# Half of each projection slot moved between a pair's two V sums, and three more weight units kept in a ring buffer

## The chip, the cores and the metric

The kernel runs on one NeuronCore of a Trainium2 chip. The metric is the device time of one execution in microseconds; the time of a kernel is the median of its runs.

## The reference

A decoder trunk of four layers works on 256 tokens of width 1024, all in float32. Layer by layer the mixer is HGRN2, FoX (softmax attention with a forget gate), Mamba-2 SSD, and HGRN2 again. Behind each mixer stands a PEER feed-forward: for each token, 8 heads pick 16 of 16384 experts by a product of keys, and each expert is one row of a table `u` and one row of a table `v`.

```python
def block(xb):                       # 128 tokens
    q = (xb @ w_q).reshape(M, 8, 2, 128)
    ...                              # top 16 of 128 x 128 sums of key scores, softmax gates
    u = jnp.take(u_tab, idx, axis=0) # (M, 8, 16, 1024)
    v = jnp.take(v_tab, idx, axis=0)
    act = gelu(einsum('md,mhkd->mhk', xb, u)) * gates
    return einsum('mhk,mhkd->md', act, v)
...
h = h + mixer(rmsnorm(h, norm_mix[i]))   # w_in, then a recurrence or attention, then w_out
h = h + peer_ffn(rmsnorm(h, norm_ffn[i]), ...)
```

So 256 tokens x 4 layers x 128 rows of 8 KB (`u` and `v` stand beside each other in memory) are gathered, 1.07 GB, and each mixer and each query projection has its weights besides.

## The kernel before

The work of one layer is split into two halves of the tokens, t=0 and t=1. There are eight stages, s = 0 to 7: stage s does the PEER of layer s//2, half s%2, and beside it, as "side work", the mixer and the queries of the next half (`side(s)` runs `ready(s + 1)`). Stage 2 thus has the FoX mixer for t=1 beside it, stage 3 the SSD mixer for t=0, stage 6 the second HGRN2 mixer for t=1.

**Pairs.** A stage has 64 pairs, 512 in all. A pair i is two gathers, g=0 and g=1. One gather (L1848, issued by POOL) brings 128 rows of 8 KB, 1 MB, into a buffer of the "ring". VectorE multiplies its `u` half with the tokens and sums (`dot`), ScalarE makes the activation and the scaled diagonal matrix (`active`: Gelu, then `dg`), and TensorE adds the `v` half into PSUM: the "V sum" (`spread`, L1919), two matmuls for each of g=0 and g=1. Behind its V sum the buffer is free, and a further gather may be issued into it. The ring holds six buffers of `gb` and, after the opening, a seventh, `GB[6]`; buffers that held kept weights join it when their weights are done.

**Weights.** A weight matrix is cut into units of 1 MB (128 x 2048 float32). `stream` lists them in the order of use, each once for t=0 and once for t=1. A unit loaded into one of NRAW = 2 `raw` buffers is loaded for both halves of the tokens. A unit named in `KEEP` goes into a kept place (`spots`, numbers 0 to 8: eight units of `kept` and the end of `mix`) and stays there for t=1. `look_ahead` and `given_back` take a kept place out of the ring when its unit is near in the stream, and hand it back when the unit has been used for the last time. Kept mixer units are loaded by a DMA that ScalarE issues (`paced`, at most PACE = 4 units ahead of use), all others by one that SyncE issues.

**The side work's slots.** A `Plan` lists for each slot n what TensorE does (`pe`) and what the other engines do behind it (`at`). `halves(ns, gen)` puts two half units of an in-projection (`project`, four matmuls of 128x512 in the order, two to a half) into one slot. `run(most)` cuts a slot in two when more than `most` us of TensorE work (3.0 for HGRN2 and FoX, 99 for SSD) by the kernel's own count have been put into it. In the main loop a pair is written in this order: `dot(i,0)`, `active(i,0)`, `spread(i,0)`, `dot(i,1)`, `active(i,1)`, `spread(i,1)`, steps of the routing, the other engines' part of the last slot (`others`), and then the next slot's TensorE work (`products_`). The next slot is taken while the counted cost is behind the line `SIDE[s] * slot / SPAN`. Engines run their instructions in the order in which they are written.

Of the kernel before, what the change touches and what calls it, by code (L numbers as in the profile page):

```python
# [26 lines left out]
UNIT = 2048  # L27
# [7 lines left out]
MIX = 10304  # L35
STAGES = 2 * DEPTH

def in_order(*units):
    return {i: k for k, i in enumerate(units)}


FIRST = in_order(*range(9))
KEEP = {"hg0": in_order(0, 1, 2, 6, 7, 8, 9, 10, 11), "hg1": {**in_order(*range(7), 8, 9), 18: 3, 19: 4}, "fox": {**in_order(0, *range(2, 10)), 15: 2},
        "ssm": {**in_order(*range(8)), 31: 0}, "wq0": in_order(3, 4, 5, 6, 1, 2, 7), "wq1": {3: 0, 4: 1, 1: 3, 2: 4, 0: 5, 5: 6, 6: 7, 7: 8},
        "wq2": {0: 1, 3: 2, 1: 3, 2: 4, 4: 5, 5: 6, 6: 7}, "wq3": {3: 0, 0: 1, 4: 2, 1: 5, 2: 6, 5: 7, 6: 8, 7: 3}}
PARKED = ({("wq0", 1): 7, ("wq0", 2): 8}, {("fox", 15): 3, ("wq1", 1): 4, ("wq1", 2): 5, ("wq1", 0): 6},
          {("ssm", 31): 0, ("wq2", 0): 1, ("wq2", 1): 3, ("wq2", 2): 4},
# [11 lines left out]
NKEPT = 8  # L59
# [146 lines left out]
def trunk(ctx: ExitStack, tc: tile.TileContext, d: dict, out: bass.AP):  # L206
# [19 lines left out]
    at_, o_ = {}, 0  # L226
# [100 lines left out]
    over = set()  # L327
    order.reverse()

    spots = [at_["kept"][:, k * UNIT:(k + 1) * UNIT] for k in range(NKEPT)] + [mix[:, MIX - UNIT:]]  # L330
    ring = deque(GB[:6])
    vacant, wanted = set(range(NKEPT + 1)), set()

# [193 lines left out]
    class Plan:  # L527
        def __init__(self):
            self.slots = {}
            self.holds = {}  # L530

        def hold(self, n, until):

# [10 lines left out]
        def halves(self, ns, gen):  # L544

            for n in ns:
                for _ in range(2):
                    self.pe(n, lambda: next(gen))

        def run(self, most):  # L550

            for n in range(max(self.slots) + 1):
                ps, fs = self.slots.get(n, ((), ()))
                while n in self.holds and routed[0] < self.holds[n]:
                    yield "wait"
                start = pe[0]
                for i, f in enumerate(ps):
                    if i and pe[0] - start > most:
                        yield
                        flush()  # L560
                        yield
                        start = pe[0]
                    f()
                yield from slot(lambda: deferred.extend(fs))

    def turned(src, use, n=4, twisted=False):

# [82 lines left out]
    def hgrn(l, t, carry):  # L650
# [147 lines left out]

        p = Plan()
        nm = "hg%d" % j  # L800
        p.halves(range(16), project(nm, ub, ["f0", "f1", "q0", "q1", "v0", "v1", "g0", "g1"]))
        if t and l:
            p.at(1, unpark, ("wq3", 0))
        p.at(1, bounds)
# [390 lines left out]
    def fox(l, t, carry):  # L1195
# [78 lines left out]
            later(lambda: nc.scalar.copy(YT[:, j], b[:, 0:P]))  # L1274

        p = Plan()
        p.halves(range(12), project("fox", ub, ["v0", "v1", "q0", "k0", "q1", "k1"]))
        p.pe(0, gate[0])
        for n in range(1, 8):
            p.at(n, lambda: next(gate[1], None))  # L1280
# [22 lines left out]
    def ssd(l, t, carry):  # L1303
# [185 lines left out]
        ins = [n for n in range(11) for _ in range(2)] + [11, 12, 13, 14, 15, 16, 17, 17, 18, 18]  # L1489
        ins += [19, 19, 20, 20, 21, 21, 22, 23, 24, 24, 25, 26, 27, 27, 28, 28]  # L1490
        gen = project("ssm", ub, list(range(8)) + ["z%d" % g for g in range(4)])
        for n in ins:
            p.pe(n, lambda: next(gen))
        p.at(0, setup)
        p.pe(1, gate[0])
        for n in range(2, 9):
# [554 lines left out]
    for s in range(STAGES):  # L2051
# [1 line left out]

            ring.extend(mix[:, (3 + 2 * i) * D:(5 + 2 * i) * D] for i in range(3))
        work = side(s) if s else chain(first, side(0))
        state = {"open": False, "done": False, "pe": 0.0, "dve": 0.0, "cost": 0.0, "slot": 0}

        def products_(force=False):

            state["slot"] += 1  # L2060
            if state["done"] or not (force or state["cost"] < SIDE[s] * state["slot"] / SPAN):
                return
            state["pe"], state["dve"] = pe[0], dve[0]
            r = next(work, work)
            state["done"] = r is work
            state["open"] = r is None
            state["pe"] = pe[0] - state["pe"]
            state["dve"] = dve[0] - state["dve"]

        def others():  # L2070

            if state["open"]:
                d0 = dve[0]
                next(work)
                state["open"] = False
                state["cost"] += max(state["pe"] / 4.6, (state["dve"] + dve[0] - d0) / 2.2, 0.5)

        for i in range(64 * s, 64 * s + 64):
# [9 lines left out]
            elif new:  # L2088

                products_(True)  # L2090
                others()
            spread(i, 0)
            if i:
                dot(i, 1)
            active(i, 1)
# [45 lines left out]
```

## Time and profile before

| | |
|---|---|
| median of 3 runs | 3025.08 us (3023.35 to 3025.86) |
| the profiled execution | 3023.55 us, of which the instructions span 3021.8 us |
| TensorE (PE), VectorE (DVE), ScalarE (ACT), GpSimd (POOL) busy | 82%, 70%, 52%, 40% |
| DMA engines | busy share 9 tenths or more in 37 of 40 slices, mean 417 GB/s |
| moved | 1259.48 MB, of it 1073.81 MB by gathers |
| ACT's table loads | 318, 1283 ns each |

The page's second part shows busy tenths in 40 slices of the span (75.5 us each) and, for the DMA engines, the GB/s that they moved. A row of a view by windows gives busy time and count of each engine, then the granted TensorE clock, the DMA engines' busy share and GB/s. A "dry spell" is here a stretch in which the GB/s fall below the 427 of a stretch with work always waiting.

### The profile page before, as it was taken

To read this page: it belongs to the slowest core of one execution; us is meant where nothing else is said; L and a number is where in the kernel's file an instruction comes from. 1 tells how busy PE (TensorE), PEld (TensorE's weight loads), DVE (VectorE), ACT (ScalarE), POOL (GpSimd) and SP (SyncE) were. 2 spreads that over 40 slices of the span, in tenths; PEclk is the share of its full clock that TensorE was granted. 3 is DMA by queue.
4 is the path that set the end of the run, shared out by engine and by line. 5 is a ranking of instruction groups with operands and counts; after the bars stand their busy time and mean duration, and the time that the engine had idled before them with its cause. 6 is when DMAs were issued, how large, how long until landed. Compare 5 with 4: busy or idle time off the path is not lost.

```text
span 3021.8 us, 35257 instructions
## 1 busy us (share of the span) xinstructions
PE 2491.9 (82%) x10583; PEld 1076.3 (36%) x10584; DVE 2123.0 (70%) x5664; ACT 1564.1 (52%) x4469; POOL 1214.9 (40%) x1040
## 2 busy tenths in 40 slices
PE   9898787887688986988779998878776888887778
PEld 7544342233134451333233443533222333431111
DVE  3877577675856867778487886787657667787755
ACT  3565444463445744577346774456444654453433
POOL 0443343444443433333344333334334443555554
PEclk9999888988799997998979999889888999999999
DMA  8899999999999999999999999999999999999998
GB/s 365 335 426 426 427 426 427 423 411 426 426 425 408 423 426 427 414 416 417 416 425 409 415 426 427 422 422 422 427 426 426 411 418 421 419 426 427 427 427 360
DMA packets 176637, 1259.48 MB, mean 417 GB/s; under 512 B 19777, under 2 KB 20161, under 8 KB 25538
## 3 DMA queue, kind: packets, MB, share of 16 engines
q0 software_dynamic: 147776, 1073.81, 84.9%
q1 hardware_dynamic: 24786, 156.13, 12.4%
q10 hardware_dynamic: 3888, 27.30, 2.2%
q8 instruction: 87, 1.43, 0.2%
q14 instruction: 100, 0.82, 0.1%
HBM read 1256.11 MB, written 1.05 MB: 416 GB/s over the span
## 4 chain that ended last, share of the span: by engine, by line
DMA 53%; PE 22%; DVE 12%; issue 7%; ACT 3%; POOL 2%; POOLq 0%; SPq 0%; DVEq 0%; ACTq 0%
DMA arena<-in_uv,ix 51%; PE pj L289 11%; DVE arena L248 8%; PE acc L1919 7%; PE ps L289 4%; POOL arena L1848 2%; DMA raw<-in_ssm 2%; ACT L261 1%; DVE eq L248 1%; ACT dg L261 1%; DVE af L248 1%; PE ps L293 1%; ACT arena L261 0%; DVE si L248 0%; DVE gs L248 0%
## 5 line engine op out<-in xcount | busy, mean ns | idle before, releaser
L1848 POOL DMA_INDIRECT arena<-in_uv,ix x1028 | 1209.5, 1177 | 1790.6 <-PE acc L1919 862.3
L248 DVE SCALAR_TENSOR_TENSOR arena<-arena 128x1024 f32<-128x1024 f32 (+2 forms) x1088 | 1265.4, 1172 | 729.1 <-DMA arena<-in_uv,ix 718.4
L1919 PE MATMUL acc<-arena,dg 128*64 128x512 f32 x4096 | 1275.3, 681 | 482.0 <-ACT dg L261 479.7
L1919 PEld LDWEIGHTS acc<-arena,dg 128*64 128x64 f32 x4096 | 285.0, 146 | 1266.3 <-ACT dg L261 985.1
L261 ACT ACTIVATE dots<-dots 128x1 f32<-128x1 f32 x896 | 177.6, 198 | 1002.0 <-DVE arena L248 999.6
L289 PE MATMUL pj<-arena 128*128 128x128 f32 (+2 forms) x2160 | 484.6, 388 | 4.7 <-DVE arena L248 4.5
L261 ACT ACT_TABLE_LOAD x318 | 408.0, 1283 | 13.4 <-DVE arena L248 6.4
L261 ACT ACTIVATE dg<-dg,dots 128x64 f32<-128x64 f32 x1024 | 356.2, 348 | 33.3
L289 PEld LDWEIGHTS pj<-arena 128*128 128x128 f32 (+1 forms) x2160 | 286.2, 190 | 201.7 <-issue 186.4
L289 PE MATMUL pj<-raw,arena 128*128 128x512 f32 (+1 forms) x736 | 313.5, 628 | 24.5 <-DMA raw<-in_ssm 20.0
L261 ACT ACTIVATE dg<-m,gs 128x64 f32<-128x64 f32 x1024 | 294.2, 335 | 1.5 <-DVE gs L248 0.8
L289 PE MATMUL ps<-arena 128*128 128x128 f32 (+5 forms) x1632 | 209.7, 282 | 1.1 <-DMA arena<-in_wq 0.7
L289 PEld LDWEIGHTS ps<-arena 128*128 128x128 f32 (+3 forms) x1632 | 170.9, 177 | 97.1 <-issue 42.7
L289 PEld LDWEIGHTS pj<-raw,arena 128*128 128x128 f32 (+1 forms) x736 | 116.0, 185 | 222.4 <-issue 183.3
L289 PE MATMUL ps<-cst,arena 128*64 128x128 f32 (+4 forms) x960 | 133.4, 321 | 5.2 <-DVE arena L248 5.2
L289 PEld LDWEIGHTS ps<-cst,arena 128*64 128x64 f32 (+1 forms) x960 | 105.7, 182 | 51.8 <-issue 32.6
L261 ACT ACTIVATE dots<-dots,rts 128x1 f32<-128x1 f32 x128 | 37.1, 290 | 137.5 <-DVE arena L248 137.4
L248 DVE DVE_READ_ACCUMULATOR arena<-arena 128x1 f32 x1024 | 84.9, 83 | 0.0
L261 ACT ACTIVATE arena<-arena 128x512 f32<-128x512 f32 (+3 forms) x88 | 49.2, 576 | 55.7 <-DVE arena L248 52.2
L261 ACT ACTIVATE arena<-ps 128x256 f32<-128x256 f32 (+3 forms) x168 | 58.5, 389 | 24.9 <-PE ps L289 24.2
L248 DVE FIND_INDEX8 si<-sv,arena 128x8 uint32<-128x128 f32 x254 | 69.3, 285 | 0.0
L293 PE MATMUL ps<-cst,arena 128*128 128x128 f32 x360 | 62.9, 299 | 3.6 <-DVE arena L248 2.4
(173 smaller groups left out, 1456.6 us busy)
## 6 DMA issues: line engine op xcount, KB each, us to landing
raw<-in_ssm SPq DMA_DIRECT2D x44, 1024.0 KB, 9.1
raw<-in_hg SPq DMA_DIRECT2D x24, 1024.0 KB, 8.9
arena<-in_hg SPq DMA_DIRECT2D x22, 1024.0 KB, 17.3
arena<-in_wq SPq DMA_DIRECT2D x20, 1024.0 KB, 9.0
arena<-in_uv,ix POOLq DMA_INDIRECT x1028, 14.5
raw<-in_wq SPq DMA_DIRECT2D x10, 1024.0 KB, 12.3
raw<-in_fox SPq DMA_DIRECT2D x10, 1024.0 KB, 9.4
arena<-in_fox ACTq DMA_DIRECT2D x9, 1024.0 KB, 9.3
```

Of the source, the lines that this page charges most:

```text
L248: return getattr(nc.vector, name)(o, *a, **k)
L261: nc.scalar.activation(o, i, f, **k)
L289: nc.tensor.matmul(o, w, m, start=start, stop=stop)
L293: nc.tensor.transpose(o, i, ident)
L1848: nc.gpsimd.indirect_dma_start(o, None, src, bass.IndirectOffsetOnAxis(ap=ix, axis=0))
L1919: nc.tensor.matmul(accs[s][e][o:o + 64], dg[:, k], v, start=hh == 0 and q == 0, stop=hh == 7 and q == NQ - 1)
```

## The change

It has two parts. First, of the two half units of an in-projection slot, the first (from slot 1 on) is no longer written in the slot, but between `spread(i, 0)` and `dot(i, 1)` of the pair ahead of it; the second stays where it was. In HGRN2 and FoX this leaves less in the slot, so `run(3.0)` cuts fewer slots in two. Second, `GB[6]` becomes place 9 for one kept unit in each of three mixers: unit 10 of FoX, unit 9 of SSD, unit 10 of the second HGRN2. While such a unit is there, the ring has one buffer less.

```diff
-KEEP = {... "hg1": {**in_order(*range(7), 8, 9), 18: 3, 19: 4}, "fox": {**in_order(0, *range(2, 10)), 15: 2},
-        "ssm": {**in_order(*range(8)), 31: 0}, ...
+KEEP = {... "hg1": {**in_order(*range(7), 8, 9), 10: 9, 18: 3, 19: 4}, "fox": {**in_order(0, *range(2, 11)), 15: 2},
+        "ssm": {**in_order(*range(8)), 9: 9, 31: 0}, ...
...
-    spots = [... for k in range(NKEPT)] + [mix[:, MIX - UNIT:]]
+    spots = [... for k in range(NKEPT)] + [mix[:, MIX - UNIT:], GB[6]]
...
+        def project(self, ns, gen):
+            for k, n in enumerate(ns):
+                if n and n not in ns[:k]:
+                    self.ahead[n] = lambda: next(gen)
+                else:
+                    self.pe(n, lambda: next(gen))
...   (Plan.run)
-                yield from slot(lambda: deferred.extend(fs))
+                deferred.extend(fs)
+                if n + 1 in self.ahead:
+                    yield "ahead"
+                    self.ahead[n + 1]()
+                yield
+                flush()
+                yield
...   (HGRN2; FoX and SSD alike)
-        p.halves(range(16), project(nm, ub, [...]))
+        p.project([n for n in range(16) for _ in range(2)], project(nm, ub, [...]))
...   (main loop)
+        def ahead():
+            if state["ahead"]:
+                p0 = pe[0]
+                next(work)
+                state["ahead"] = False
+                state["pe"] += pe[0] - p0
...
             spread(i, 0)
+            ahead()
             if i:
                 dot(i, 1)
```

What this does to the order shows in three places. In the rows, `acc<-arena,dg` is a V sum (x4 is a whole pair, x2 one half of it), `pj<-arena` 128x512 a projection (x2 is one half unit), `ps` all other TensorE work of the side; V sums are L1919 before and L1933 in the change.

TensorE, the beginning of the SSD in-projection for t=0 (stage 3), before:

```order
491 L1919 MATMUL acc<-arena,dg 64x512 x4
492 L289 MATMUL pj<-arena 128x512 x4
493 L1919 MATMUL acc<-arena,dg 64x512 x4
494 L289 MATMUL pj<-arena 128x512 x4
495 L289 MATMUL ps<-par,arena 128x32 x8
496 L1919 MATMUL acc<-arena,dg 64x512 x4
497 L289 MATMUL pj<-arena 128x512 x4
```

and the same place in the change:

```order
544 L1933 MATMUL acc<-arena,dg 64x512 x4
545 L289 MATMUL pj<-arena 128x512 x4
546 L1933 MATMUL acc<-arena,dg 64x512 x2
547 L289 MATMUL pj<-arena 128x512 x2
548 L1933 MATMUL acc<-arena,dg 64x512 x2
549 L289 MATMUL pj<-arena 128x512 x2
550 L289 MATMUL ps<-par,arena 128x32 x8
551 L1933 MATMUL acc<-arena,dg 64x512 x2
552 L289 MATMUL pj<-arena 128x512 x2
```

Two of the four projection matmuls have moved in front of the pair's second V sum.

TensorE, the beginning of the second HGRN2's in-projection for t=1 (stage 6), before:

```order
957 L1919 MATMUL acc<-arena,dg 64x512 x4
958 L289 MATMUL pj<-arena 128x512 x4
959 L1919 MATMUL acc<-arena,dg 64x512 x4
960 L289 MATMUL pj<-arena 128x512 x4
961 L1919 MATMUL acc<-arena,dg 64x512 x4
962 L289 MATMUL ps<-cst,arena 128x128 x8
963 L289 MATMUL pj<-arena 128x512 x4
964 L1919 MATMUL acc<-arena,dg 64x512 x4
965 L289 MATMUL ps<-arena 128x128 x16
966 L1919 MATMUL acc<-arena,dg 64x512 x4
967 L289 MATMUL pj<-arena 128x512 x4
```

and in the change:

```order
1123 L1933 MATMUL acc<-arena,dg 64x512 x4
1124 L289 MATMUL pj<-arena 128x512 x4
1125 L1933 MATMUL acc<-arena,dg 64x512 x2
1126 L289 MATMUL pj<-arena 128x512 x2
1127 L1933 MATMUL acc<-arena,dg 64x512 x2
1128 L289 MATMUL pj<-arena 128x512 x2
1129 L1933 MATMUL acc<-arena,dg 64x512 x2
1130 L289 MATMUL pj<-arena 128x512 x2
1131 L1933 MATMUL acc<-arena,dg 64x512 x2
1132 L289 MATMUL ps<-cst,arena 128x128 x8
1133 L289 MATMUL pj<-arena 128x512 x2
1134 L289 MATMUL ps<-arena 128x128 x16
```

The work of rows 962 to 967 took two slots with a pair between them; rows 1132 to 1134 are one slot. From here to the first 32x32 products of this mixer there are 16 pairs before and 11 in the change.

SyncE, the weight loads around FoX, t=0 and then t=1, as a difference (`raw` is a buffer for one use, `arena` anything else, `in_wq` query weights, `in_keys` the keys):

```order
-L1975 DMA arena<-in_keys 128x1024
-L443 DMA raw<-in_fox 128x2048 x5
+L1989 DMA arena<-in_keys 128x1024
+L443 DMA raw<-in_fox 128x2048 x4
 L441 DMA arena<-in_fox 128x1024 x2
 L441 DMA arena<-in_wq 128x1024 x2
 L443 DMA raw<-in_wq 128x2048 x2
 L443 DMA arena<-in_wq 128x2048 x2
-L1592 DMA arena<-in_keys 128x1024
-L443 DMA raw<-in_fox 128x2048 x2
+L1606 DMA arena<-in_keys 128x1024
+L443 DMA raw<-in_fox 128x2048
```

One load of 1 MB is gone in t=0 (ScalarE issues it now, so its DMAs go from 27 to 30 over the three mixers) and one in t=1 (nobody issues it). In all SyncE's DMAs go from 174 to 168. ScalarE's table loads go from 318 to 335, since other functions stand between its Gelus; the matmuls are the same number.

More of the change, by code (lines that the diff above doesn't have):

```diff
@@ L42 @@
 FIRST = in_order(*range(9))
-KEEP = {"hg0": in_order(0, 1, 2, 6, 7, 8, 9, 10, 11), "hg1": {**in_order(*range(7), 8, 9), 18: 3, 19: 4}, "fox": {**in_order(0, *range(2, 10)), 15: 2},
-        "ssm": {**in_order(*range(8)), 31: 0}, "wq0": in_order(3, 4, 5, 6, 1, 2, 7), "wq1": {3: 0, 4: 1, 1: 3, 2: 4, 0: 5, 5: 6, 6: 7, 7: 8},
+KEEP = {"hg0": in_order(0, 1, 2, 6, 7, 8, 9, 10, 11), "hg1": {**in_order(*range(7), 8, 9), 10: 9, 18: 3, 19: 4}, "fox": {**in_order(0, *range(2, 11)), 15: 2},
+        "ssm": {**in_order(*range(8)), 9: 9, 31: 0}, "wq0": in_order(3, 4, 5, 6, 1, 2, 7), "wq1": {3: 0, 4: 1, 1: 3, 2: 4, 0: 5, 5: 6, 6: 7, 7: 8},
         "wq2": {0: 1, 3: 2, 1: 3, 2: 4, 4: 5, 5: 6, 6: 7}, "wq3": {3: 0, 0: 1, 4: 2, 1: 5, 2: 6, 5: 7, 6: 8, 7: 3}}
@@ L328, in trunk @@
     order.reverse()
-    spots = [at_["kept"][:, k * UNIT:(k + 1) * UNIT] for k in range(NKEPT)] + [mix[:, MIX - UNIT:]]
+    spots = [at_["kept"][:, k * UNIT:(k + 1) * UNIT] for k in range(NKEPT)] + [mix[:, MIX - UNIT:], GB[6]]
     ring = deque(GB[:6])
@@ L530, in __init__ @@
             self.holds = {}
+            self.ahead = {}
         def hold(self, n, until):
@@ L800, in hgrn @@
         nm = "hg%d" % j
-        p.halves(range(16), project(nm, ub, ["f0", "f1", "q0", "q1", "v0", "v1", "g0", "g1"]))
+        p.project([n for n in range(16) for _ in range(2)], project(nm, ub, ["f0", "f1", "q0", "q1", "v0", "v1", "g0", "g1"]))
         if t and l:
@@ L1276, in fox @@
         p = Plan()
-        p.halves(range(12), project("fox", ub, ["v0", "v1", "q0", "k0", "q1", "k1"]))
+        p.project([n for n in range(12) for _ in range(2)], project("fox", ub, ["v0", "v1", "q0", "k0", "q1", "k1"]))
         p.pe(0, gate[0])
@@ L1491, in ssd @@
         gen = project("ssm", ub, list(range(8)) + ["z%d" % g for g in range(4)])
-        for n in ins:
-            p.pe(n, lambda: next(gen))
+        p.project(ins, gen)
         p.at(0, setup)
@@ L2055, in trunk @@
         work = side(s) if s else chain(first, side(0))
-        state = {"open": False, "done": False, "pe": 0.0, "dve": 0.0, "cost": 0.0, "slot": 0}
+        state = {"open": False, "done": False, "ahead": False, "pe": 0.0, "dve": 0.0, "cost": 0.0, "slot": 0}
         def products_(force=False):
@@ L2065, in products_ @@
             state["done"] = r is work
-            state["open"] = r is None
+            state["ahead"] = r == "ahead"
+            state["open"] = r is None or state["ahead"]
             state["pe"] = pe[0] - state["pe"]
             state["dve"] = dve[0] - state["dve"]
+        def ahead():
[4 more added lines that the diff above has]
+                state["pe"] += pe[0] - p0
         def others():
+            ahead()
             if state["open"]:
@@ L2092, in trunk @@
             spread(i, 0)
+            ahead()
             if i:
```

## The prediction

> **What bounds the kernel now.** I read first the page's slices and queues, then the chain that ended last, then stretches of the span by windows, and at last who waits for whom.
>
> ```profile
> span 3021.8 us, 35257 instructions
> ...
> PE 2491.9 (82%) x10583; PEld 1076.3 (36%) x10584; DVE 2123.0 (70%) x5664; ACT 1564.1 (52%) x4469; POOL 1214.9 (40%) x1040
> ...
> DMA  8899999999999999999999999999999999999998
> GB/s 365 335 426 426 427 426 427 423 411 426 426 425 408 423 426 427 414 416 417 416 425 409 415 426 427 422 422 422 427 426 426 411 418 421 419 426 427 427 427 360
> ...
> DMA 53%; PE 22%; DVE 12%; issue 7%; ACT 3%; POOL 2%; POOLq 0%; SPq 0%; DVEq 0%; ACTq 0%
> ...
> L261 ACT ACT_TABLE_LOAD x318 | 408.0, 1283 | 13.4 <-DVE arena L248 6.4
> ...
> arena<-in_uv,ix POOLq DMA_INDIRECT x1028, 14.5
> ...
> raw<-in_fox SPq DMA_DIRECT2D x10, 1024.0 KB, 9.4
> arena<-in_fox ACTq DMA_DIRECT2D x9, 1024.0 KB, 9.3
> ```
>
> No engine is full, the DMA engines are: apart from the first two slices and the last one they move 408 to 427 GB/s, and 427 is the most that any slice reaches. 53% of the chain that ended last is DMA. So the time is bytes over 427 GB/s, and what is lost below that. What could be won besides bytes are the dry spells.
>
> I cut the span into stretches of 20 us and joined neighbours under 412 GB/s. These are all such spells between 120 and 3000 us; the last row is one of the stretches with nothing lost, for comparison.
>
> ```profile
> 640.00:680.00 40.00, 33.34 (x142) 13.25 (x142) 29.63 (x85) 28.70 (x81) 19.29 (x16) 0.91 1.00 399
> 1240.00:1280.00 40.00, 37.03 (x122) 13.85 (x122) 37.81 (x118) 24.30 (x69) 14.18 (x12) 1.00 0.99 403
> 1320.00:1360.00 40.00, 33.59 (x119) 13.36 (x120) 28.71 (x87) 23.29 (x63) 14.31 (x12) 0.91 1.00 405
> 1400.00:1460.00 60.00, 51.55 (x210) 21.48 (x210) 48.27 (x108) 40.48 (x101) 22.68 (x19) 0.91 0.99 401
> 1600.00:1640.00 40.00, 40.00 (x140) 17.10 (x138) 26.96 (x69) 26.38 (x66) 17.60 (x14) 0.96 0.99 394
> 2020.00:2060.00 40.00, 34.12 (x106) 14.01 (x108) 27.03 (x77) 26.29 (x60) 13.51 (x13) 0.91 0.99 409
> 2380.00:2440.00 60.00, 52.72 (x205) 22.67 (x206) 39.88 (x97) 46.46 (x116) 24.31 (x22) 1.00 0.99 398
> 940.00:980.00 40.00, 40.00 (x193) 22.24 (x192) 24.82 (x67) 22.19 (x64) 13.17 (x12) 0.99 0.97 392
> 1680.00:1720.00 40.00, 40.00 (x218) 24.28 (x218) 30.33 (x90) 32.35 (x77) 11.54 (x10) 0.98 1.00 404
> 2560.00:2580.00 20.00, 18.47 (x73) 6.32 (x73) 13.60 (x30) 10.48 (x35) 8.27 (x6) 1.00 0.96 378
> 2920.00:2940.00 20.00, 15.01 (x32) 3.72 (x32) 9.71 (x15) 6.08 (x23) 9.58 (x9) 1.00 1.01 427
> ```
>
> The columns are length, busy time of PE, weight loads, DVE, ACT and POOL, then clock, DMA share, GB/s. A spell's loss is its length times (427 - GB/s)/427: 2.6, 2.2, 2.1, 3.7, 3.1, 1.7, 4.1, 3.3, 2.1 and 2.3 us, 27.2 in all. In three of them PE is busy 40.00 of 40 us. Who holds the gathers back then is in the waits, and what the pair looks like is in the order of time on PE:
>
> ```profile
> POOL arena L1848 <- PE acc L1919: 862.3, 369, 12.1
> POOL arena L1848 <- DVE arena L248: 302.3, 114, 12.8
> ```
>
> ```profile
> PE acc L1919 <- ACT dg L261: 479.7, 385, 5.4
> ```
>
> ```profile
> 1254.12 1.94 PE L1919 MATMUL acc<-arena,dg 128*64 128x512 f32 x8 [0.31 <-ACT dg L261]
> 1255.99 3.70 PE L289 MATMUL pj<-arena 128*128 128x512 f32 x8
> 1259.62 1.94 PE L1919 MATMUL acc<-arena,dg 128*64 128x512 f32 x8
> ```
>
> A gather waits above all for a V sum, because that frees its buffer. Both V sums of a pair run back to back (1.94 us), then comes the slot's projection (3.70 us), and no buffer is freed until the next pair: two free within 2 us and then none for some 4 us. Elsewhere PE waits 479.7 us in 385 pieces for the diagonal matrix that it needs, 1.25 us each.
>
> **The change, part by part.** (1) *Three loads of 1 MB less*, in t=1 of FoX, SSD and the second HGRN2. 1.0486 MB at 427 GB/s are 2.46 us, three are 7.4 us. Where the DMA engines are full this comes off the time whole; where PE sets the pace it is worth nothing. Between 0 and 7.4 I take 7.4: 417 GB/s is the mean over the whole span, and even the worst of the ten spells still moves 378. Three loads in t=0 go from SP's queue to ACT's. Both kinds land in the same time (9.4 and 9.3 us in the page's rows), and the place is free some pairs before ACT comes to the issue, so ACT does not stand still for it: nothing.
>
> (2) *One ring buffer less*, from the time its unit is near in t=0 until it is used up in t=1. By the order this is from pair 73 to 146, 197 to 267 and 327 to 402, which are these stretches of the trace:
>
> ```profile
> 526.60:931.40 404.80, 318.03 (x1243) 120.05 (x1242) 273.17 (x725) 198.21 (x604) 173.42 (x148) 0.89 1.01 423
> 1214.10:1656.30 442.20, 370.35 (x1464) 152.38 (x1463) 322.38 (x873) 261.09 (x699) 169.38 (x144) 0.92 1.00 416
> 2033.70:2451.00 417.30, 333.85 (x1280) 123.46 (x1280) 283.14 (x710) 222.50 (x631) 178.36 (x153) 0.89 1.01 420
> ```
>
> Seven of the ten spells, the first seven rows above, lie in them. With one buffer fewer a spell begins up to 1 MB earlier, so it loses up to 2.46 us more: 7 x 2.46 = 17.2 us at most. At least it is nothing, where the queue holds out; a gain is excluded, since fewer buffers let no gather start sooner. No row shows a ring of six (in these stretches it is seven throughout). A gather takes 14.5 us from issue to landing and 1 MB moves in 2.46, so some five or six stand in the queue at a time: a spell needs a burst of several microseconds to begin. I take five of the seven, 12.3 us, leaving out the two with the least PE work (33.34 and 33.59 of 40 us).
>
> (3) *Half of the slot between the V sums.* PE does the same matmuls. The last burst of a pair is shorter by half of 3.70, 1.85 us, so the next pair's first buffer comes free up to 1.85 us sooner, while the second V sum, which often waits for its matrix anyway, comes later by at most as much. In the spells where PE is not full and the slot is an in-projection (1240, 1320, 1400, 2020, 2380) that is worth up to the smaller of 1.85 and the spell's own loss: 4 x 1.85 + 1.7 = 9.1 us. Where PE is busy 40.00 of 40, another order frees nothing sooner on the whole, and at 640 and 2560, by the order, no in-projection stands. Ends: 0, and all that the five and the two full in-projection spells 1600 and 1680 lose, 2.2 + 2.1 + 3.7 + 1.7 + 4.1 + 3.1 + 2.1 = 19.0. I take 9.1.
>
> (4) *Fewer slots cut in two.* The side work comes in fewer pairs. In the second HGRN2, t=1, the order puts into 11 pairs what stood in 16. These 16 are:
>
> ```profile
> 2366.30:2457.00 90.70, 81.63 (x316) 34.58 (x316) 55.32 (x128) 58.89 (x152) 36.41 (x33) 1.00 1.00 408
> ```
>
> ```profile
> 2366.30:2457.00 90.70, 31.19 (x128) 7.57 (x128) 1.00 1.00 408
> ```
>
> The first row is all of PE's work, the second the V sums alone: the side work is 81.63 - 31.19 = 50.4 us, a pair's V sums 1.95. Eleven pairs then need 50.4 + 21.4 = 71.8 us of PE. Their 22 gathers and the six MB of loads that the order puts there need 28 x 2.46 = 68.9 of DMA. PE is the longer by 2.9 us. The first HGRN2 and FoX in t=1 are packed alike, so up to 3 x 2.9 = 8.7 us are lost; at least 0, as a queue of five gathers covers 2.9 us. I take 0; if that cover is gone because the ring is shorter, the loss falls into the spells that (2) has counted. The 17 further table loads are 17 x 1.283 = 21.8 us of ACT, which is busy 52% of the time; where one stands ahead of a Gelu in a full stretch, the V sum is late by it, which has the same cover.
>
> Sum: -7.4 + 12.3 - 9.1 + 0 = -4.2 us. The profiled execution took 3023.55 us (1.75 around its span), the median is 1.5 above it; I put the sum on the median: 3025.08 - 4.2 = **3020.9 us**. For this kernel 0.2%, 6 us, is about what a measurement can tell from no change.
>
> **The rivals.** *The dips close.* The queue holds out with six buffers, (2) costs nothing, (3) gives its 9.1: 3025.08 - 7.4 - 9.1 = 3008.6. For it speaks that the first V sum is what the gathers wait for longest, against it that in seven spells the ring has less to give.
>
> *The ring of six runs dry* (the other side). The place is the three stretches above. Each of their seven spells loses its whole 2.46 us more and the half slots return nothing, since a late second V sum holds its buffer as much longer as the first gives it back sooner: -7.4 + 17.2 = +9.8, 3034.9. It decides from (7.4 + 6.05)/2.46 = 5.5 spells on; at three spells the bytes are eaten up. For it: 416 GB/s in the middle stretch, where the ring of seven is already too short.
>
> *The bytes are worth nothing*, because PE sets the pace in t=1, and the rest is as I sum it: +12.3 - 9.1 = +3.2, 3028.3. For it only 1600 and 940 us with PE at 40.00 of 40; against it 420 and more GB/s in most slices.
>
> *The moved loads hold up gathers.* On the rows above a load lands in 9.3 to 9.4 us and a gather in 14.5: a load goes past gathers that were issued before it. If a load on ACT's queue runs beside one on SP's, a gather waits for one more MB, three times 2.46 us: -4.2 + 7.4 = +3.2, 3028.3. Against it: ACT issues such loads before too (9 of FoX alone), without a spell of their own. The Trainium skill, page "DMA: Bandwidth & Descriptors", section "Queues, rings and completion order", says that each DMA engine goes round between the queue rows that have work, a packet at a time; SP, ACT and the gathers have a row each. By that rule a third row at work takes a gather's share from a half to a third, which is this rival, and the landing times agree with its first half; no row shows the three at once.
>
> **How the numbers follow.** My sum has 0.44 (3015 to 3026; 0.18 of it faster by over 0.2%, 0.26 within), the closing dips 0.22 (faster), the dry ring 0.23 (0.21 slower, 0.02 within), the worthless bytes 0.06 and the held-up gathers 0.05 (both within). So faster 0.40, within 0.2% 0.39, slower 0.21. The range goes from 3008, the closing dips, to 3033, most of the dry ring: 0.07 lies under it, 0.12 above.
>
> **What would show it.** (1): 1256.3 MB in all instead of 1259.48, and SP's and ACT's queues together three loads shorter. (2): GB/s of the three stretches; below 416 in the middle one the ring is dry. (3): in an in-projection pair one V sum of about 1 us, 1.85 us of projection, the second V sum, 1.85 us more; fewer us in "POOL waits for PE acc". (4): the HGRN2 slots of t=1 in some 11 pairs, with PE full there and GB/s under 408. I am wrong if the three stretches together lose 6 us more or 12 us less than the sum has it.

## The result, and the profile after

The change made the kernel slower. Its median is 3048.49 us (3044.43 to 3051.64, 6 runs) against 3024.22 us of before on the same chip (3022.41 to 3026.54, 6 runs): ratio 1.008, 95% interval 1.0067 to 1.0092, so 20 to 28 us more, some 24. Forecast were 3020.9 us and a range up to 3033.

From the page of the changed kernel, the lines that answer to those of before:

```profile
span 3049.3 us, 35288 instructions
...
PE 2532.4 (83%) x10584; PEld 1054.5 (35%) x10584; DVE 2122.4 (70%) x5664; ACT 1588.6 (52%) x4496; POOL 1221.3 (40%) x1040
...
GB/s 363 338 394 426 426 427 427 409 401 417 426 409 410 427 426 426 421 409 419 420 424 399 423 409 427 408 404 425 416 427 426 380 376 427 426 426 427 427 427 357
DMA packets 176205, 1256.33 MB, mean 412 GB/s; under 512 B 19729, under 2 KB 20113, under 8 KB 25490
...
L261 ACT ACT_TABLE_LOAD x335 | 429.8, 1283 | 13.7 <-DVE arena L248 6.5
...
arena<-in_uv,ix POOLq DMA_INDIRECT x1028, 12.9
```

3.15 MB less are moved, as the change says, but at 412 GB/s instead of 417. Apart from the first two slices and the last, the lowest are the third (394, stage 0) and the two at 2.36 to 2.52 ms (380 and 376, stage 6); before they had 426, 411 and 418. Two things are new that nothing in the diff counts. PE is busy 40.5 us longer with the same matmuls (2532.4 against 2491.9); part of that can be the trace's, since e3 and e8 below, with the order of before on PE, have 2486.9 and 2507.0. And a gather lands 12.9 us after its issue instead of 14.5; in e3 and e8, which have of the change only the three units' place in the ring, it is 13.4 and 13.3, so most of that comes with the shorter ring.

The three stretches in which the ring has one buffer less, within a pair or two those of before; then stages 4, 6 and 0 of the change, and stages 0 and 6 of before (windows; columns as above):

```profile
536.00:955.50 419.50, 338.83 (x1312) 128.99 (x1310) 278.88 (x749) 211.13 (x626) 164.18 (x147) 0.89 1.00 413
1223.00:1664.90 441.90, 374.78 (x1457) 145.06 (x1456) 320.03 (x867) 262.10 (x697) 166.22 (x143) 0.93 1.00 415
2044.80:2490.20 445.40, 362.08 (x1336) 129.17 (x1336) 291.22 (x741) 237.52 (x652) 167.84 (x155) 0.87 0.98 404
```

```profile
1589.80:1998.70 408.90, 366.90 (x1666) 170.36 (x1667) 303.69 (x839) 240.93 (x644) 150.43 (x130) 0.94 1.00 414
...
2361.80:2728.80 367.00, 312.23 (x1405) 137.19 (x1405) 253.65 (x659) 192.44 (x552) 162.37 (x134) 0.90 0.98 406
108.20:472.90 364.70, 306.79 (x1408) 135.75 (x1409) 263.86 (x723) 204.57 (x554) 157.62 (x131) 0.91 1.00 420
```

```profile
108.10:467.20 359.10, 301.44 (x1409) 137.16 (x1409) 264.52 (x724) 196.91 (x544) 151.06 (x131) 0.92 1.01 426
2346.70:2701.20 354.50, 300.08 (x1405) 138.56 (x1405) 253.45 (x664) 187.38 (x547) 153.80 (x133) 0.94 1.01 419
```

From stage 0 to stage 6 the change's trace is longer by 5.6, 3.2, 0.0, 0.2, 4.9, 1.1 and 12.5 us, which is the 27.5 by which the span grew: nearly half of it falls in stage 6.

By length x (427 - GB/s)/427 the three stretches lose 13.8, 12.4 and 24.0 us, 50 in all, against 3.8, 11.4 and 6.8, 22 in all, before: 28 us more where the sum had about 3. Stage 0, where the ring is as long as before, loses 6.0 instead of 0.8. So a shorter ring cannot be the whole of it.

Who waits for whom:

```profile
POOL arena L1862 <- PE acc L1933: 935.8, 418, 6.8
```

```profile
PE acc L1933 <- ACT dg L261: 473.4, 389, 5.2
```

The gathers wait 73.5 us longer for V sums (862.3 before), though the half slots were to free buffers sooner.

### The profile page after: what moved, and what is told of

It is laid out like the page before. It is cut to its first block, busy times and chain, and to the rows that moved or that the text cites. A ratio compares the mean times of both kernels' runs of the same rounds, so it can differ in the third digit from the quotient of the medians.

```text
span 3049.3 us, 35288 instructions
## 1 busy us (share of the span) xinstructions
PE 2532.4 (83%) x10584; PEld 1054.5 (35%) x10584; DVE 2122.4 (70%) x5664; ACT 1588.6 (52%) x4496; POOL 1221.3 (40%) x1040
## 2 busy tenths in 40 slices
DMA packets 176205, 1256.33 MB, mean 412 GB/s; under 512 B 19729, under 2 KB 20113, under 8 KB 25490
## 4 chain that ended last, share of the span: by engine, by line
DMA 52%; PE 20%; DVE 15%; issue 7%; ACT 3%; POOL 2%; POOLq 0%; SPq 0%; DVEq 0%; ACTq 0%
DMA arena<-in_uv,ix 51%; DVE arena L248 10%; PE pj L289 10%; PE acc L1933 6%; PE ps L289 4%; POOL arena L1862 2%; ACT L261 1%; DVE eq L248 1%; ACT dg L261 1%; DMA raw<-in_ssm 1%; DVE af L248 1%; DVE si L248 1%; ACT arena L261 1%; PE ps L293 0%; DVE sv L248 0%
## 5 line engine op out<-in xcount | busy, mean ns | idle before, releaser
L1862 POOL DMA_INDIRECT arena<-in_uv,ix x1028 | 1215.8, 1183 | 1811.9 <-PE acc L1933 935.8
L248 DVE SCALAR_TENSOR_TENSOR arena<-arena 128x1024 f32<-128x1024 f32 (+1 forms) x1088 | 1264.1, 1171 | 722.2 <-DMA arena<-in_uv,ix 711.0
L1933 PE MATMUL acc<-arena,dg 128*64 128x512 f32 x4096 | 1314.0, 693 | 475.5 <-ACT dg L261 473.4
L1933 PEld LDWEIGHTS acc<-arena,dg 128*64 128x64 f32 x4096 | 278.3, 147 | 1300.3 <-ACT dg L261 1003.6
L289 PE MATMUL pj<-arena 128*128 128x128 f32 (+2 forms) x2208 | 528.8, 398 | 5.0 <-DVE arena L248 4.9
L289 PE MATMUL pj<-raw,arena 128*128 128x512 f32 (+1 forms) x688 | 293.3, 624 | 17.3 <-DMA raw<-in_ssm 15.6
L289 PEld LDWEIGHTS pj<-raw,arena 128*128 128x128 f32 (+1 forms) x688 | 100.6, 179 | 204.4 <-issue 174.2
## 6 DMA issues: line engine op xcount, KB each, us to landing
arena<-in_hg SPq DMA_DIRECT2D x22, 1024.0 KB, 16.6
arena<-in_uv,ix POOLq DMA_INDIRECT x1028, 12.9
```

What stands on the lines that cost most here:

```text
L248: return getattr(nc.vector, name)(o, *a, **k)
L289: nc.tensor.matmul(o, w, m, start=start, stop=stop)
L1862: nc.gpsimd.indirect_dma_start(o, None, src, bass.IndirectOffsetOnAxis(ap=ix, axis=0))
L1933: nc.tensor.matmul(accs[s][e][o:o + 64], dg[:, k], v, start=hh == 0 and q == 0, stop=hh == 7 and q == NQ - 1)
```

## The experiments

All differences are against before on the same chip, as ratio x 3024 us with its 95% interval. The theories at the start: A, slots that are cut less often are too full (a "full slot" does in one pair what took two); B, the ring of six runs dry; C, the half slot makes the second V sum late. The first four runs take the change apart.

**e1, fewer cuts alone.**

```diff
-        p.halves(range(16), project(...))      # HGRN2; FoX alike
+        p.halves(range(16), project(...), True)
...
-                    if i and pe[0] - start > most:
+                    if i and pe[0] - start > most + (1.74 if n and n in self.pairs else 0.0):
```

> Only the cutting of the slots is that of the change: an in-projection slot of HGRN2 and FoX may hold 1.74 us (by the kernel's count) more before it is cut in two, which gives the same fewer and fuller slots; both halves stay behind the second V sum, no unit more is kept, the ring stays at seven. In the second HGRN2, t=1, single pairs then have up to 10.9 us of side matmuls where before none had more than 6.7. Theory A (full slots: a burst of PE longer than the queue of gathers covers, term 4 of the prediction mis-sized): +12 to +22 us against before. Theory B (dry ring of six, term 2): this kernel loses at most the 6 us that the change lost in stage 0, where its ring was seven: 0 to +6 us. Theory C (the half slot makes the second V sum late): 0.

1.0034 (1.0022 to 1.0047): +10.3 us (+6.7 to +14.2). A part of the change that leaves the order within a pair and the bytes as they were makes nearly half of the loss; B and C have no place for that, and A had it a little larger.

**e2, half slots alone.** The change without the kept units, and with the half that stands ahead counted in, so that the cuts are those of before:

```diff
-                start = pe[0]
+                start = pe[0] - (1.74 if n in self.ahead else 0.0)
```

> Only the half slots: the first half of an in-projection slot stands between the pair's two V sums, but the slots are cut in two where before cut them (the half that stands ahead is counted in), no unit more is kept, the ring stays at seven. Prediction's term 3: -9 us (0 to -19). Theory A (full slots): 0 to -9 us. Theory B (dry ring): 0 to -9 us. Theory C (the half slot makes the second V sum late, so that the second buffer comes free later by what the first wins): +5 to +15 us.

1.0035 (1.0022 to 1.0049): +10.6 us (+6.7 to +14.8). Within C's bounds, outside A's, B's and the prediction's. The order of time on PE in an in-projection of e2 shows what the pair has become:

```profile
1260.45 1.08 PE L1933 MATMUL acc<-arena,dg 128*64 128x512 f32 x4
1261.46 1.98 PE L289 MATMUL pj<-arena 128*128 128x512 f32 x4
1263.37 1.08 PE L1933 MATMUL acc<-arena,dg 128*64 128x512 f32 x4
1264.38 1.98 PE L289 MATMUL pj<-arena 128*128 128x512 f32 x4
1266.29 1.08 PE L1933 MATMUL acc<-arena,dg 128*64 128x512 f32 x4
```

It is the order that the change says, and PE doesn't stand still in it. But from one pair's first V sum to the next it takes 5.84 us (1266.29 - 1260.45), where before it took 5.50 (1259.62 - 1254.12 in the prediction's rows) with the same eight matmuls of each kind. PE now changes four times a pair between V sums and projections instead of twice, so a change costs 0.17 us. A change of operands and of the PSUM bank alone has no such price. In before,

```profile
1249.66 3.70 PE L289 MATMUL pj<-arena 128*128 128x512 f32 x8
1253.19 0.62 PE L293 MATMUL ps<-cst,arena 128*128 128x128 f32 x4
```

it is 3.53 us from the start of the projection to that of other products on 128*128 tiles (1253.19 - 1249.66), and 3.63 where a V sum on 128*64 tiles follows (1259.62 - 1255.99). The price goes with the change of tile.

That makes a theory D: the price of the changes, which falls on the end where PE is the bound and is hidden where the DMA engines are. Stage 4, the SSD mixer for t=1, in windows of before, e2 and e6 (below):

```profile
1580.70:1984.70 404.00, 359.10 (x1667) 177.19 (x1667) 303.30 (x839) 239.69 (x644) 149.39 (x129) 0.93 1.01 420
```

```profile
1579.80:1998.10 418.30, 370.32 (x1667) 172.10 (x1668) 303.47 (x839) 239.83 (x644) 146.66 (x129) 0.93 0.99 405
```

```profile
1580.10:1995.50 415.40, 368.87 (x1667) 171.50 (x1668) 303.40 (x839) 239.80 (x644) 150.84 (x129) 0.93 1.00 409
```

The same 1667 matmuls take 11 us more of PE in e2 at the same granted clock (0.93), and the stage is 14.3 us longer. By count it is 28 half slots x 0.34 = 9.5 us. PE stands still for 44.9 us of the stage in before, 48.0 in e2 and 46.5 in e6: what PE has more comes nearly whole on top.

**e3, kept units alone.**

```diff
+  KEEP and spots as in the change; slots, cuts and order of before
```

> Only the kept units: three units stay in the seventh ring buffer, three loads of 1 MB less, the ring is one shorter in the three stretches; slots and their order as before. Prediction's terms 1 and 2: +4.9 us (-7.4 to +9.8). Theory A (full slots): -7 to +5 us, since without the bursts the shorter queue holds out. Theory B (dry ring): +12 to +24 us. Theory C: -7 to +5 us.

1.0005 (0.9996 to 1.0014): +1.5 us (-1.2 to +4.2). B falls: the ring of six with the bytes it saves costs next to nothing.

**e4, half slots and fewer cuts, nothing kept.**

```diff
-  KEEP and spots of the change
+  KEEP and spots of before
```

> The change without the kept units: half slots and the change's fewer cuts, ring of seven throughout and the bytes of before. Theory A (full slots): +6 to +20 us against before; with the kept units' cost it adds up to the change's 24. Theory B (dry ring): -9 to +6 us. Theory C: +5 to +15 us, the same as the half slots alone within 3 us.

1.0071 (1.0058 to 1.0085): +21.5 us (+17.5 to +25.7), the sum of e1 and e2. With e3 it makes 23 of the change's 24.

**e5 and e6, half slots in one half of the tokens** (cuts of before):

```diff
-                if n and n not in ns[:k]:
+                if early and n and n not in ns[:k]:      # early: t == 0 in e5, t == 1 in e6
```

> Half slots with the cuts of before, as in e2, but only in the mixers for t=0 (54 of the 123 in-projection slots); ring, kept units and bytes of before. Theory C (the second V sum comes late, everywhere alike): 54/123 of e2's +10, so +3 to +6 us. Theory D (each half slot makes TensorE change twice more between V sums and projections, 5.84 us a pair in e2's trace against 5.50 before, so 0.34 us, which costs where TensorE is the bound and is hidden where the DMA engines are): in t=0 most weights are loaded, 7.4 us of DMA a pair against 5.84, so the 18 us more of TensorE are hidden, and the gain that e2's trace shows in stage 3 (lost 2.4 us against 9.1) stays: -8 to +1 us.

0.9995 (0.9985 to 1.0004): -1.5 us (-4.5 to +1.2). As D has it, C's +3 to +6 is excluded. The 54 x 0.34 = 18 us that PE has more by count are hidden, but nothing measurable is won.

> The counterpart of e5: half slots with the cuts of before only in the mixers for t=1 (69 slots, 28 of them in stage 4). Theory C: 69/123 of e2's +10, so +4 to +7 us. Theory D: in t=1 most units are kept, a pair has 4.9 us of gathers beside 5.84 of TensorE, so that the price falls on the end: 28 x 0.34 = 9.5 us in stage 4 at least, up to 69 x 0.34 = 23 us in all: +9 to +20 us, nearly all of it in stage 4.

1.0032 (1.0020 to 1.0044): +9.7 us (+6.0 to +13.3), all of e2's loss. The row above has stage 4 at 415.4 us, 11.4 longer, with 9.8 us more of PE.

**e7, the whole slot between the V sums.**

```diff
-                if n and n not in ns[:k]:
-                    self.ahead[n] = lambda: next(gen)
+                if n:
+                    self.ahead[n] = self.ahead.get(n, ()) + (lambda: next(gen),)
```

> Both halves of an in-projection slot stand between the pair's two V sums, with the cuts of before; ring, kept units and bytes of before. In HGRN2 and FoX this is a rotation: the second V sum of a pair and the first of the next stand together, TensorE changes no oftener than before, but the second V sum stands 3.7 us behind the first; in SSD, where other matmuls follow in the slot, it changes as often as with half slots. Theory C: twice e2's, +16 to +24 us, and losses in all stages from 0 to 6. Theory D: HGRN2 and FoX as before, stage 4 as in e2: +5 to +13 us.

1.0041 (1.0027 to 1.0055): +12.4 us (+8.2 to +16.6). The time is D's, the places are not. Stages 4 and 6:

```profile
1580.10:1988.00 407.90, 365.36 (x1667) 169.24 (x1668) 303.92 (x839) 240.13 (x644) 148.39 (x129) 0.94 1.01 416
```

```profile
2349.50:2712.10 362.60, 303.98 (x1404) 140.19 (x1405) 254.48 (x663) 187.86 (x549) 153.10 (x132) 0.92 0.99 413
```

In stage 4, where the second V sum comes later than in e2, PE has 6.3 us more instead of 11.2 and the stage is 3.9 us longer instead of 14.3: a V sum that is later still costs less, so there it is not the late V sum that costs. (D had this stage as in e2, which isn't met either.) In stage 6, where D expected nothing, the stage is 8 us longer than the 354.5 of before. That fits a second V sum that is 3.7 us late, but it is one trace, no run tells it apart from other causes, and in the order of before this stage takes 352.4 to 359.4 us from trace to trace (e13, e12). Second V sums that are 1.85 us late cost nothing measurable (e5, e10). So C can hold for the whole slot only.

**e8, the ring of six without the saving.**

```diff
-                elif rs is not r and (nm, i) not in kept:
+                elif rs is not r and ((nm, i) not in kept or k == NKEPT + 1):    # on top of e3
```

> The ring alone: as e3, the three units have their place in the seventh ring buffer, which is out of the ring in the three stretches, but they are loaded again into it for t=1, so that the bytes are those of before. Prediction's term 2: +12.3 us (0 to 17.2). With e3's +1.5 and bytes worth 7.4: +8.9. If bytes are worth nothing where TensorE has more to do than the DMA engines (t=1, the place where they are saved): +1.5.

1.0024 (1.0015 to 1.0034): +7.3 us (+4.5 to +10.3). Less e3's 1.5 the bytes are worth 5.8 us of the 7.4; with both intervals that is some 2 to 10. The three stretches of e8, pair for pair those of before:

```profile
527.40:931.30 403.90, 320.57 (x1243) 121.58 (x1242) 272.65 (x725) 197.95 (x604) 171.22 (x148) 0.88 1.00 419
1213.90:1656.10 442.20, 373.10 (x1455) 152.40 (x1454) 317.26 (x858) 258.92 (x692) 173.89 (x142) 0.91 1.00 412
2038.70:2463.40 424.70, 337.22 (x1282) 125.13 (x1282) 285.13 (x711) 223.00 (x631) 177.55 (x154) 0.88 1.00 414
```

By the formula of above they lose 36 us against 22 before. So the shorter ring alone makes about half of the 28 us that the stretches lost in the change, while the whole kernel is only 7.3 us slower; outside the stretches it must lose less than before.

**e9, e1 with a flatter pace.**

```diff
-SIDE = (47, 31, 45, 55, 100, 35.2, 46, 1.8)
+SIDE = (42, 28, 40, 55, 100, 31.5, 41, 1.8)
```

> As e1 (the change's fewer cuts alone), but the line that sets the pace of the side work is flatter in the HGRN2 and FoX stages (SIDE 42, 28, 40, 31.5, 41 for 47, 31, 45, 35.2, 46), so that the side work reaches its middle and its end in the pairs in which it did before, or up to four later. What is left of e1 is the full single slots. Theory A1 (it is the single full slots of up to 9.7 us, longer than the queue covers): as e1, +6 to +12 us, with stage 6 losing its 14 us again. Theory A2 (it is that the side work as a whole comes earlier, in fewer pairs): -3 to +4 us, with stage 6 at 6 to 9 us.

1.0052 (1.0038 to 1.0065): +15.7 us (+11.5 to +19.7), no better than e1. That the side work as a whole comes early (A2) is excluded; it is the full single slots, at a higher price than A1 said; whether the flatter pace adds to it in this order was not run apart. What in them costs it is told apart by e13 to e16.

**e10, half slots everywhere but in the SSD mixer for t=1.**

```diff
-        p.project(ins, gen)
+        p.project(ins, gen, t == 0)                # on top of e2, SSD
```

> As e2 (half slots, cuts of before), but the SSD mixer for t=1, the one whose in-projection has the most for TensorE to do, keeps its slots whole: 95 of the 123 half slots are left. Theory C (late second V sums): 95/123 of e2's +10: +5 to +10 us. Theory D (TensorE's changes, paid in stage 4): stage 4 is as before, so -2 to +4 us.

1.0004 (0.9995 to 1.0013): +1.2 us (-1.5 to +3.9). Without 28 of its 123 half slots e2's loss is gone. C's +5 to +10 is excluded.

**e11, two changes more and nothing moved.**

```diff
+        def change():
+            nc.tensor.matmul(bank()[0:64, 0:64], cst[:, 0:64], cst[:, 0:64], start=True, stop=True)
...
+            if t and n and n not in ins[:k] and n in ins[k + 1:]:
+                p.pe(n, change)
```

> The price of a change alone: the order of before, no V sum and no projection moved, but in the SSD mixer for t=1 one matmul of 128x64 weights by 64 columns into an unused bank stands between the two halves of each of 22 in-projection slots, which makes TensorE change twice more in such a pair. Its result isn't used. Theory D: 22 x (0.34 + about 0.1 for the matmul itself) = 9.7 us more of TensorE in stage 4, of which stage 4 passes on most: +5 to +10 us. Theory C: no V sum stands behind anything more than half a microsecond: 0 to +2 us.

1.0012 (1.0003 to 1.0021): +3.6 us (+0.9 to +6.4). There are 18 such slots, not 22. Rows of PE in e11, and its stage 4:

```profile
1644.74 1.98 PE L289 MATMUL pj<-arena 128*128 128x512 f32 x4
1646.66 0.33 PE L1494 MATMUL ps<-cst 128*64 128x64 f32 x2
1646.92 1.98 PE L289 MATMUL pj<-arena 128*128 128x512 f32 x4
1648.74 0.60 PE L293 MATMUL ps<-cst,arena 128*128 128x128 f32 x4
```

```profile
1583.20:1991.20 408.00, 364.07 (x1703) 176.34 (x1704) 303.41 (x839) 239.72 (x644) 148.44 (x129) 0.94 1.00 417
```

From the start of the first half to that of the products behind the second it is 4.00 us (1648.74 - 1644.74) instead of 3.53 (the rows of before under e2), so 0.47 us for one small matmul and its two changes. PE has 5.0 us more in the stage and the stage is 4 us longer, without a V sum having moved. But 18 x 0.47 would be 8.5, and stage 4 in the order of before takes 404.0 to 407.3 us from trace to trace (e9, e12), so the stage's own 408 says little. The time lies between D's bounds and C's and decides nothing between them; being clear of zero, it fits D, in that more time of PE costs something where no V sum has moved far.

**e12, a flatter pace alone** (SIDE 44, 30, 42, 52, 100, 33, 43 in before):

> Before with a flatter pace of the side work (SIDE 44, 30, 42, 52, 100, 33, 43), the slots cut as before: the reverse of what the change did, and a version that could beat before. Theory A2 (the side work as a whole comes too early): -6 to -1 us. Theory A1 (single full slots): -2 to +3 us, since the fullest slots stay as they are.

1.0001 (0.9992 to 1.0010): +0.3 us (-2.4 to +3.0). The pace is worth nothing, as A1 has it.

**e13 to e16: which engine is too full in a full slot?** ScalarE in e1, where stage 6 dips, in order of time; then windows of before and of e1, 20 us of stage 6's dip and 20 us of stage 0's each:

```profile
2404.42 1.28 ACT L261 ACT_TABLE_LOAD   x1
2405.72 1.06 ACT L261 ACTIVATE arena<-arena 128x1024 f32<-128x1024 f32 x1
2406.68 1.98 ACT L356 COPY arena<-arena 128x1024 f32<-128x1024 f32 x2
2408.67 1.28 ACT L261 ACT_TABLE_LOAD   x1
2409.97 0.20 ACT L261 ACTIVATE spare<-eps 128x1 f32<-128x1 f32 x1
...
2411.61 1.28 ACT L261 ACT_TABLE_LOAD   x1
```

```profile
2400.00:2420.00 20.00, 17.16 (x56) 5.91 (x56) 15.80 (x48) 17.71 (x37) 9.41 (x8) 1.00 0.99 389
...
170.00:190.00 20.00, 19.42 (x85) 9.24 (x85) 16.60 (x52) 16.21 (x38) 8.85 (x7) 1.00 1.01 425
```

```profile
2400.00:2420.00 20.00, 17.52 (x53) 6.68 (x53) 14.69 (x38) 19.65 (x41) 5.57 (x5) 1.00 0.88 323
...
170.00:190.00 20.00, 18.36 (x65) 7.68 (x66) 16.70 (x51) 19.64 (x46) 7.50 (x8) 1.00 0.94 374
```

A pair with a full slot takes ScalarE 7.19 us (2404.42 to 2411.61), against 4.9 of DMA: a table load for the mixer's function, its work, a copy of a parked weight unit, a table load back for the next Gelu, and the pair's own 1.6 us. It stands in front of the pair's `dg`, and so of its V sums. In before, from 2410 us on, a pair with none of this stands behind each such pair; in e1 five come one behind the other. In both dips of e1 ScalarE is busy 19.6 of 20 us. The Trainium skill, page "ScalarE: Activation LUTs", section "Table sets: the hidden batching unit", says to batch calls by table set; each full slot of HGRN2 goes to another set and back once, which these rows show at 2 x 1.28 us a pair.

```diff
-            nc.scalar.copy(spots[k][...], parked.pop((unit, e)))             # e13: before; e14: e1
+            nc.vector.tensor_copy(spots[k][...], parked.pop((unit, e)))
...
-            act(K[:, sl[g]], ub.pop("f%d" % g), AF.Sigmoid)                  # e15: before; e16: e1
+            act(K[:, sl[g]], ub.pop("f%d" % g), AF.Tanh)                     # so Exp and Ln; Sqrt -> Identity
```

> Before, with the copies of parked weights into their kept places (30 copies of 128x1024, 1.05 us each, two to a unit) on VectorE instead of ScalarE. Theory A-ACT (the dips of the HGRN2 stages come from ScalarE, which is 17 to 19 of 20 us busy in before's dip of stage 6 too): that dip gets smaller, -4 to 0 us. Theory A-PE (TensorE's bursts): 0 to +2 us.

> e1 (fewer cuts alone) with the copies of parked weights on VectorE instead of ScalarE. In the dip of stage 6 three pairs of some 7 us of ScalarE each have two such copies, 2.0 us a pair. Theory A-ACT: the loss of stage 6 falls from 14 to 8 to 10 us, the whole to +2 to +7 us against before. Theory A-PE: as e1, +7 to +14 us.

> Before with other functions in the HGRN2 mixers: Tanh for Exp, Sigmoid and Ln, and Identity for Sqrt, which need no table of their own (49 of the 318 table loads fall away); the values are thus others, all matrices, sizes and the order on TensorE are those of before. It is the base for e16. Theory A-ACT: 49 x 1.28 = 63 us less of ScalarE, of it some in the dips of stages 0 and 6: -6 to 0 us. Theory A-PE: -2 to +1 us.

> e1 (fewer cuts alone) with the functions of e15 in the HGRN2 mixers, so without their table loads; TensorE's bursts of up to 9.7 us between two V sums are as in e1. Theory A-ACT: a pair in the dips has 2.6 us less of ScalarE (4.6 to 5.5 instead of 7.2 to 8.1, against 4.9 of DMA), so that the fewer cuts cost next to nothing any more: -3 to +4 us against e15, stages 0 and 6 as in e15. Theory A-PE: +7 to +14 us against e15, with stage 6 losing its 14 us.

e13: 0.9999 (0.9990 to 1.0009), -0.3 us. e14: 1.0015 (1.0006 to 1.0025), +4.5 us (+1.8 to +7.6). e15: 1.0000 (0.9991 to 1.0009). e16: 1.0008 (0.9999 to 1.0017), +2.4 us (-0.3 to +5.1). So with less on ScalarE the fewer cuts cost 2 to 5 us instead of 10, with TensorE's bursts as they were. Stage 6 in windows of e1, e14, e15 and e16:

```profile
2346.40:2710.60 364.20, 307.73 (x1404) 139.76 (x1404) 256.12 (x669) 192.80 (x552) 155.84 (x133) 0.91 0.99 411
```

```profile
2349.30:2704.50 355.20, 304.20 (x1405) 139.78 (x1405) 260.99 (x669) 183.29 (x542) 155.08 (x132) 0.92 1.01 419
```

```profile
2349.10:2702.60 353.50, 301.65 (x1404) 138.61 (x1404) 253.53 (x664) 167.56 (x526) 155.95 (x133) 0.93 1.01 421
```

```profile
2350.50:2706.20 355.70, 304.79 (x1405) 140.02 (x1405) 254.07 (x659) 167.71 (x526) 152.76 (x132) 0.92 1.01 419
```

Stage 6 goes from 364.2 us back to 355, by either way of taking work off ScalarE: there it was ScalarE. In stage 0 e16 still dips, and now PE alone is full; the second row is the whole stage:

```profile
170.00:190.00 20.00, 20.00 (x72) 7.96 (x71) 16.90 (x51) 14.97 (x45) 10.83 (x8) 1.00 0.96 364
...
112.30:471.10 358.80, 302.95 (x1409) 139.74 (x1410) 262.36 (x717) 177.13 (x525) 152.63 (x131) 0.91 1.01 420
```

The ring there is of seven, no half slot stands there, and ScalarE has 5 us to spare: PE's burst is what is left for the dip. But the stage as a whole takes 358.8 us against 359.1 in before (it begins 4 us later, as it does in e11 and e12), so that PE's burst cost time there is not shown. What the remaining 2 to 5 us are stays open; in e16 they are not clear of nothing.

**e17, the change with its causes taken out.**

```diff
+                start = pe[0] - (1.74 if n in self.ahead else 0.0)
+        p.project(ins, gen, t == 0)                                          # SSD
+            nc.vector.tensor_copy(spots[k][...], parked.pop((unit, e)))
```

> The change with the two causes of its loss taken out: the slots are cut in two where before cut them, the SSD mixer for t=1 keeps its slots whole, and the copies of parked weights are on VectorE; the three kept units and the other 95 half slots stay. If the prices add up: e3's +1.5, e10's +1.2 and e13's 0 make +2.7, -2 to +7 us against before. If the parts together cost something of their own (a ring of six with half slots): +8 to +15 us. The prediction's sum of its terms 1 to 3 was -4.2.

1.0006 (0.9997 to 1.0015): +1.8 us (-0.9 to +4.5), as the parts add up; a ring of six and half slots together cost nothing of their own that could be measured. No version that ran is measurably faster than before.

## Why the prediction was wrong

The median lies 27.6 us above the forecast. Term 3 is off by 19.7 us, term 4 by 10.3; terms 1 and 2 together give 3.4 back; these make 26.6, and the last 1 us is within the intervals. The ring, of which the prediction was most afraid, cost less than the sum had. Two steps failed: term 3 took the two halves of a slot to cost PE no more than the whole, and term 4 priced a full slot on PE and DMA and not on ScalarE.

- *Term 1, bytes* (-7.4): 1256.33 MB as said, worth 5.8 us by e8 less e3. Right within what these two runs can tell.
- *Term 2, ring* (+12.3, bounds 0 to 17.2): +7.3 in e8. The mechanism was right, the stretches do lose more with a shorter ring; five dry spells at a whole megabyte each was too much for the time, three is what it cost. Terms 1 and 2 together +4.9, measured +1.5. The stretches' GB/s, named as the sign, don't measure that time: with the ring alone they fall to 419, 412 and 414 (e8), 14 us more lost where the kernel is 7.3 slower, and in the change to 413, 415 and 404 with the other two parts on top.
- *Term 3, half slots* (-9.1, bounds 0 to -19): +10.6 in e2. The step that failed is "PE does the same matmuls. The last burst of a pair is shorter by half of 3.70". A half isn't half of the whole. Before's own trace has halves that stand alone, one of a projection's shape between two V sums and one of a V sum:

```profile
2418.25 1.98 PE L289 MATMUL ps<-cst,arena 128*128 128x512 f32 x4
2420.16 1.94 PE L1919 MATMUL acc<-arena,dg 128*64 128x512 f32 x8
...
2453.14 1.08 PE L1919 MATMUL acc<-arena,dg 128*64 128x512 f32 x4 [1.00 <-ACT dg L261]
2454.15 3.70 PE L289 MATMUL pj<-arena 128*128 128x512 f32 x8
```

  From start to start the first takes 1.91 us, twice that is 3.82 where the whole projection takes 3.63 (1259.62 - 1255.99); the second takes 1.01, twice 2.02 where the whole V sum takes 1.87 (1255.99 - 1254.12). Together that is 0.34 us a pair, as e2 has it. The Trainium skill, page "TensorEngine Tiling (Array Packing)", section "Key Properties", says that changing the tiling mode drains the engine; the rows name the modes, 128*64 for V sums and 128*128 for projections, and the price of a change in e2, e6 and e11 agrees, though no row shows the drain itself. By before's rows alone the worse end of term 3 was not 0 but a loss of 28 x 0.34 = 9.5 us in stage 4, where PE has 359 us of work in 404. The prediction did see that PE is full at 1600 and 1680 and that "another order frees nothing sooner"; it did not ask whether another order takes longer. The gain, too, was not there: e5 and e10, without stage 4's price, are within -4.5 and +3.9.
- *Term 4, fewer cuts* (0, bounds 0 to 8.7): +10.3 in e1. The burst was costed on PE only, and its 17 table loads were given "the same cover". Priced as stated, on the pair, it would have been seen: two table loads, the slot's functions, the copy and the Gelu chain are 7.2 us of ScalarE in a pair of 4.9 us of DMA, and the prediction's own row for 2380 to 2440 has ACT busy 46.46 of 60 us. 52% over the span hid that. In stage 6, which is 9.7 us longer in e1's trace, ScalarE was the cause (e14, e16); that PE's burst in stage 0 cost anything is not shown. The prediction took 0 with a cover that does not hold for such pairs in a row.
- *The rivals.* The dry ring gave the right side by the wrong mechanism: it cost 7.3 us, three spells' worth, where it would have decided from 5.5 on. None of the five cases had a price for the half slot itself or for ScalarE in a full slot; so the range ended 15 us short.
- *What would show it.* The bytes and the V sum of about 1 us came as said. "Fewer us in POOL waits for PE acc" did not: 935.8 against 862.3. The middle stretch has 415 GB/s, just under the 416 named as the sign of a dry ring, and 412 with the ring alone. The HGRN2 slots of t=1 were to have PE full and GB/s under 408; this window of the changed kernel has 312, far under it, with PE not full and ACT busy 46.52 us. The granted clock is 0.94 there, where the prediction's row of this dip has 1.00; what that costs by itself no run shows.

```profile
2400.00:2460.00 60.00, 55.33 (x205) 23.35 (x204) 35.04 (x90) 46.52 (x107) 17.09 (x16) 0.94 0.85 312
```

  The prediction was to be wrong from 6 us more in the three stretches on; they lost 25 more than the sum had.

Left open: how much of stage 4's added PE time reaches the end. The half slots made that stage 418.3, 415.4 and 413.2 us long in e2, e6 and e4, but 408.9 in the change, where one load less falls in it, and e11 with 5.0 us more of PE ended 3.6 later. Also open is what the first V sum's sooner buffer is worth where PE has room: e5's -1.5 doesn't show it apart from nothing.

## What to carry to other kernels

Before a group of matmuls is split, look in the trace for the same group standing alone: the difference between twice the half and the whole, from start to start, is the price of the split (0.34 us a pair here), and it falls due in the stage in which TensorE is the bound, not in the mean. Before work is packed into fewer steps, add up each engine's time in one full step, ScalarE's table loads there and back among it, and set it beside the DMA time of that step: an engine at 52% of the span can be at 98% for 20 us, and it is that stretch which pays. Where several edits go together, run them apart; here the part that was to gain and the part that looked free cost nearly all of it.

## What the runs showed of the hardware that was not expected

A change between matmuls of 128*64 and 128*128 tiles costs 0.17 us (5.84 - 5.50 us for two more in e2), also where nothing waits; going on to other operands and another bank on the same 128*128 tiles shows no such price (3.53 us from start to start against 3.63 in before). Second V sums that are late by 1.85 us cost nothing measurable (e5, -1.5; e10, +1.2); the one run in which they are late by 3.7 us has a stage 6 that is 8 us longer (e7), without it being shown that the late V sum is why. A ring of six instead of seven buffers of 1 MB over 1260 us of the span cost 7.3 us (e8).
